# The opening of a hybrid encoder block on one core: a fixed order, block b11 of four token tiles first, two products of the second weight group brought forward, the normalised rows made twice instead of stored

## The chip, the core and the metric

The kernel runs on one core of one Trainium2 chip, in one launch. The metric is device time in microseconds; the median of three runs of the kernel before is 2131.55 us (2130.61 to 2132.82).

A core has TensorE (PE in the profile: matrix products and transposes, which accumulate into eight PSUM banks), VectorE (DVE), ScalarE (ACT) and GpSimd (POOL), each with its own instruction stream that is carried out in order, and DMA queues. In this kernel nearly all loads, and many stores, are issued by SyncE (SP), some by ACT.

## The reference, cut to what matters here

```python
h = layer_norm(x, ln_in_g, ln_in_b)          # x: 1024 tokens x 1024, fp32
proj = h @ w_in[l]                            # 1024 x (many column tiles of 128)
aq, ak, av, hq, hf_fwd, hf_bwd, hi, hg, ga, gh = jnp.split(proj, split_idx, axis=-1)
att = dilated_attention(aq, ak, av, slopes)
rec = hgrn2(hq, hf_fwd, hf_bwd, hi, hg, lower_bounds[:, l], hgrn_norm_g[l])
merged = sigmoid(ga) * (att @ w_att_up[l]) + sigmoid(gh) * (rec @ w_hgrn_up[l])
h = layer_norm(DEEPNORM_ALPHA * h + merged @ w_o[l], ln1_g[l], ln1_b[l])
gate, up = jnp.split(h @ w_ffn_in[l], 2, axis=-1)
h = layer_norm(DEEPNORM_ALPHA * h + (silu(gate) * up) @ w_ffn_out[l], ln2_g[l], ln2_b[l])
```

The change touches the first two lines, and the `DEEPNORM_ALPHA * h` of the first residual.

## The kernel before

**Phase 1** computes the transposed projection with a Winograd form of Strassen's product. The normalised and transposed x is a 2 x 2 matrix of blocks: b11 and b21 hold tokens 0 to 511 (token tiles 0 to 3), b12 and b22 hold tokens 512 to 1023 (tiles 4 to 7); b11 and b12 hold features 0 to 511, b21 and b22 the others. Four combinations are made: t1 = b12 - b11, t2 = b22 - t1, t3 = b22 - b12, t4 = b21 - b11 - t3 (which is b21 - t2). Each of the seven right-hand operands is kept as two fp32r tiles, a high part (a cast on ACT, L205) and a low part (a subtraction, L209, on DVE here). The weights of each *weight group* (four column tiles of 128, in two pairs g = 0 and 1) are loaded as blocks a11, a12, a21 and a22, and combined into s1 to s4.

**A product** is one of seven per pair and group, in the order a11·b11, a12·b21, s2·t2, s1·t1, s3·t3, s4·b22, a22·t4 (`ORDER` and `PRODUCTS`: 1, 2, 6, 5, 7, 3, 4), pair 0 and pair 1 of each in turn. It runs over four tiles of 128 features, and each takes three matmuls of 128 x 512 (`mm3`, L244 to L246): high by high, high by low, low by high. So a product is 12 matmuls.

**`stream` (L457)** is a generator that issues these products, one at each call. `block` loads a weight block on SP (L453) into a buffer of its own name and pair; there is one buffer for each, so a block of the next group is loaded once the last reader of the present one is done. `sums` makes s1 (L477, DVE), s3 (L478, POOL), s2 (L479, DVE) and s4 (L482, DVE) in place, five products ahead. `prep` splits a product's weights into high (ACT) and low (POOL) three products ahead. `keep` (L500) copies a partial sum out of PSUM on ACT, and the evacuations `plain`, `tanhs` and `silu2` (L390 to L420) add a kept sum to another one on DVE and store the outcome.

**`phase0` (L287)** prepares x, tile by tile: load (SP), statistics (L191 and L198 on DVE, epsilon L199 on DVE, power L200 on POOL), normalisation (L266 on DVE and L267 on ACT, the whole tile of 128 x 1024 at once), a store of the normalised rows `ah` through ACT's DMA queue (L317), then for each half of the features four transposes (L274, PE) into one PSUM bank, whose copies out (L282 on ACT, L284 on DVE) apply gain and offset. A tile of the first four fills its columns of b11 and of b21; a tile of the last four gives t1 and t2, and a loop at the end makes t3, b22 and t4 of those four tiles. `phase1` (L1088) lets it run for four tiles, then issues two products, then the rest of it; the products that follow come from the main loop of `phase1`, which mixes them with the attention and the recurrence (HGRN, L884 on).

**What sets the order.** Instructions are issued in the order in which the program issues them, but a list scheduler that simulates a timeline puts them into each engine's stream by priority and due time; `tc.high_priority(offset=evac_ahead)` raises evacuations and weight preparation.

**`residual` (L352)** runs much later, between two stretches of the last weight groups. For each token tile it loads the stored rows `ah` (L360, SP), scales them and adds the offset (L361 and L362, DVE), and stores the outcome (ACT's queue) for the first residual addition.

The lines of `residual`, `tanhs` and of the loop that calls `phase0` that the change and the steps touch:

```python
            nc.sync.dma_start(a, self.ah_d[tt])
            nc.vector.scalar_tensor_tensor(a, a, ALPHA, gb, op0=OP.mult, op1=OP.mult)
            nc.vector.scalar_tensor_tensor(a, bb, ALPHA, a, op0=OP.mult, op1=OP.add)
...
        work = self.stream(tiles)
            norm = self.phase0(p0)
            for _ in range(4):
                next(norm)
            for _ in range(2):
                next(work)
            for _ in norm:
                pass
```

Of the kernel before, what the change touches and what calls it, by code (L numbers as in the profile page):

```python
# [19 lines left out]
D = 1024  # L20
# [54 lines left out]
CST_PAD = 160  # L75
# [4 lines left out]
class Block:  # L80
    evac_ahead = 1000

    def __init__(self, ctx, tc, x, ln_in_g, ln_in_b, w_in, hgrn_lb, hgrn_norm_g, w_att_up, w_hgrn_up,
# [28 lines left out]
        self.ah_d = scratch("ah", 8)  # L112
# [25 lines left out]
    def consts(self):  # L138
# [20 lines left out]
        self.my = take(64).bitcast(I32)  # L159
        self.mhalf = cst.tile([128, 8], F32, name="mhalf")  # L160
        nc.vector.memset(self.mhalf, -0.5)

    def columns(self, pool):

        nc = self.nc
        rows = pool.tile([128, 128], F32, name="vrows")
        at, r = {}, 0
        for name, src, n in (("gin", self.ln["in"][0], 8), ("bin", self.ln["in"][1], 8), ("g1", self.ln["1"][0], 8),
                             ("b1", self.ln["1"][1], 8), ("lb", self.lbw, 32), ("ng", self.ng, 1)):
            nc.scalar.dma_start(rows[r:r + n, :], bass.AP(tensor=src.tensor, offset=src.offset, ap=[[128, n], [1, 128]]))  # L170
            at[name] = r
            r += n
        ps = self.ps_sd()
        nc.tensor.transpose(ps[:, :r], rows[:r, :], self.ident[:r, :r])
        a, b = self.cst.tile([128, 32], F32, name="vc"), self.cst1.tile([128, 33], F32, name="vc1")
        nc.vector.tensor_copy(a, ps[:, 0:32])
        nc.vector.tensor_copy(b, ps[:, 32:65])
        self.col = {n: a[:, at[n]:at[n] + 8] for n in ("gin", "bin", "g1", "b1")}
        self.lbraw, self.ngraw = b[:, 0:32], b[:, 32:33]

# [106 lines left out]
    def phase0(self, pool):  # L287


        nc, kept, rest = self.nc, [], []  # L290

        def hold(n):
            t = pool.tile([128, D], F32, name=n, tag="xt", bufs=7)
            return t, [t[:, HALF * i:HALF * (i + 1)].rearrange("p (k c) -> p k c", k=4) for i in range(2)]

        xs = []

        def load():
            tt = len(xs)
            if tt < 8:  # L300
                xs.append(hold("xt"))
                for h in range(2 if tt == 0 else 1):
                    s = slice(HALF * h, HALF * (h + 1)) if tt == 0 else slice(0, D)
                    nc.sync.dma_start(xs[tt][0][:, s], self.x[128 * tt:128 * (tt + 1), s])

        for tt in range(8):
            for _ in range(4 if tt == 0 else 1):
                load()
            xt, (t1, t2) = xs[tt]
            if tt == 0:  # L310
                self.columns(pool)
                gc, bc = self.col["gin"], self.col["bin"]
            if tt == 1:
                self.rest()
# [5 lines left out]
            def put(name, v, c=c):  # L320
                hi, lo = self.xb[name]
                self.split(hi[:, :, c], lo[:, :, c], v, eng_lo="dve")

            if tt < 4:
                v = [self.half3("v11"), self.half3("v21") if tt == 0 else
                     pool.tile([128, 4, 128], F32, name=f"v21{tt}")]
                kept.append(v)
                for q, n in enumerate(("b11", "b21")):
                    self.transposed(pool, xt, q, gc, bc, v[q], on_act=(1, 3, 4, 6))
                    put(n, v[q])  # L330
                yield
                continue
            b11, b21 = kept[tt - 4]
            _, (b12, b22) = hold("vt")
            self.transposed(pool, xt, 0, gc, bc, b12, on_act=(0, 1, 3))
            nc.vector.tensor_sub(t1, b12, b11)
            put("t1", t1)
            self.transposed(pool, xt, 1, gc, bc, b22, on_act=(4, 5, 7))
            nc.vector.tensor_sub(t2, b22, t1)
            put("t2", t2)  # L340
            rest.append((put, b12, b22, b21, b11))

        for put, b12, b22, b21, b11 in rest:
            nc.vector.tensor_sub(b12, b22, b12)
            put("t3", b12)
        for put, b12, b22, b21, b11 in rest:
            put("b22", b22)
        for put, t3, b22, b21, b11 in rest:
            nc.vector.tensor_sub(b21, b21, b11)
            nc.vector.tensor_sub(b21, b21, t3)  # L350
            put("t4", b21)

    def residual(self, pool, vecs):
# [95 lines left out]
    def block(self, n, g, name):  # L449

        t = self.blk.tile([128, 4, 128], F32, name=f"w{name}", tag=f"{name}{g}", bufs=1)
        c, r = self.cols[4 * n + 2 * g + int(name[1]) - 1], HALF * (int(name[2]) - 1)
        self.nc.sync.dma_start(t, self.w_in[r:r + HALF, c:c + 128].rearrange("(k p) c -> p k c", p=128))  # L453
        return t

    def stream(self, tiles):
# [3 lines left out]
        seq = [(n, g, p) for n in range(len(tiles) // 4) for p in self.ORDER for g in range(2)]  # L460
        after = {6: "a11", 7: "a21", 3: "a12", 4: "a22"}
        A = [{b: self.block(0, g, b) for b in ("a11", "a12", "a21", "a22")} for g in range(2)]
        state = [{}, {}]
        ready = {}

        def early(n):
            return tc.high_priority(offset=self.evac_ahead if n else 0)
# [27 lines left out]
        def bank(n, g, b):  # L495
            return self.ps_pj(2 * g + (n + b) % 2)
# [6 lines left out]
        for i in range(3):  # L503
            prep(i)
        for i, (n, g, p) in enumerate(seq):
            if i == 2:
                for j in range(4, 7):
                    sums(j)
                prep(4)
            if i >= 2:  # L510
                sums(i + 5)
            if i != 1:
                prep(i + 3)
            s = state[g]
            if p in (1, 2):
                s[p] = bank(n, g, p)
# [6 lines left out]
            pair = [f for _, f in tiles[4 * n + 2 * g:4 * n + 2 * g + 2]]  # L523
            with tc.high_priority(offset=self.evac_ahead):
                if p in (1, 6):
                    s["u"] = keep(ps, f"k1{g}")
                elif p == 5:
                    s["m5"] = keep(ps, f"k5{g}")
                elif p == 2:
                    pair[0](0, ps, s["u"])  # L530
                elif p == 7:
                    pair[1](1, ps, s["m5"])
                elif p == 3:
                    pair[0](1, ps, s["u"])
                else:
                    pair[1](0, ps, None)
# [551 lines left out]
    def phase1(self):  # L1088
# [12 lines left out]
        work = self.stream(tiles)  # L1101
        with self.pool("p0") as p0:
            norm = self.phase0(p0)
            for _ in range(4):
                next(norm)
# [620 lines left out]
```

## Time and profile before

| | |
|---|---|
| median of three runs | 2131.55 us |
| span of the profiled execution (no other time of it is recorded) | 2135.9 us |
| mean granted TensorE clock of that execution | 0.985 |
| TensorE busy in 84 to 200 us | 111.1 of 116 |
| TensorE busy in 200 to 1160 us | 929.2 of 960 |
| TensorE busy in 1160 to 1260 us, where the residual rows are made | 93.5 of 100 |
| TensorE busy from 1260 us on | 855.4 of 876 |

The span goes from the first to the last instruction of one profiled execution. It lies 4.3 us (0.2%) above the median of the runs, so numbers out of the trace are compared with numbers out of the trace, and differences are carried over to the median.

A row of the timeline gives the start in us, the duration in us, the engine, the line of the program, the operation, out<-in by the program's names, the tile's shape and type, and how many instructions the row holds; in brackets stands how long the engine was idle before, and which engine, tile and line released it. Matmuls overlap: a row's duration is that of its pipeline, and the distance between two starts is what one costs. Several instructions of one line in a row are put together (x8), and their duration then holds small gaps too. A row of the groups gives busy time and the mean in ns of one instruction, then the idle time ahead of such instructions and what ended most of it. A row of the windows gives the stretch, its length, then busy time and instruction count of PE, PE's weight loads, DVE, ACT and POOL, the granted clock, the share of the DMA engines' time and GB/s. Names in the trace are those of the buffers: `pj` and `sd` are PSUM banks, `wa` a weight block, `ws` a sum, `xt` and `vt` rows of x, `v` a transposed half tile, `evh` an evacuated half row.

### The profile page before, as it was taken

What the parts mean: (1) busy time and instruction counts of PE and PEld (TensorE: products, weight loads), DVE (VectorE), ACT (ScalarE), POOL (GpSimd) and SP (SyncE); (2) the same over time, 40 slices, a digit from 0 to 9 for tenths busy, and PEclk for the clock granted to TensorE, in tenths of its full rate; (3) what the DMA queues carried; (4) which work ended last, traced back from release to release, by engine and by line L of the source; (5) the groups of instructions that cost most, each with busy time, mean ns of one, the idle gap of its engine ahead of it and who ended that gap; (6) DMA issues with size and microseconds to landing.
All of it is one profiled execution on the core that took longest, in us unless ns stands there. A gap on an engine that the chain in (4) does not pass through costs nothing.

```text
span 2135.9 us, 30950 instructions
## 1 busy us (share of the span) xinstructions
PE 2032.5 (95%) x10941; PEld 1678.8 (79%) x10941; DVE 1386.7 (65%) x2228; ACT 918.9 (43%) x1864; POOL 1090.4 (51%) x882
## 2 busy tenths in 40 slices
PE   4799999999999999989999899999999999999998
PEld 3678787878878888868888688878788888888876
DVE  7666746776468754677536722336867677767777
ACT  6544445444554435443355332134433333334542
POOL 3465653565535764466644764353656666630012
PEclk9899999999999999999999999999999999999999
DMA  5343452434424453333433855244434334348433
GB/s 206 103 125 103 131 159 89 141 110 150 140 90 139 129 170 122 121 118 114 156 111 117 286 191 185 87 138 143 148 109 158 129 130 142 119 153 305 158 89 124
DMA packets 273885, 301.10 MB, mean 141 GB/s; under 512 B 14081, under 2 KB 205378, under 8 KB 273730
## 3 DMA queue, kind: packets, MB, share of 16 engines
q1 hardware_dynamic: 266272, 273.73, 39.9%
q10 hardware_dynamic: 7458, 25.40, 3.0%
q8 instruction: 86, 1.41, 0.3%
q14 instruction: 69, 0.57, 0.1%
HBM read 200.25 MB, written 98.83 MB: 140 GB/s over the span
## 4 chain that ended last, share of the span: by engine, by line
PE 62%; DVE 6%; issue 3%; DMA 3%; POOL 2%; ACT 1%; SPq 0%; ACTq 0%; DVEq 0%; POOLq 0%
PE pj L244 13%; PE pj L245 13%; PE pj L246 13%; PE sd L245 6%; PE sd L244 6%; PE sd L246 6%; POOL w_lo L209 1%; PE sd L1038 1%; PE sd L987 1%; DMA a<-ah 1%; DVE qd L956 1%; DVE qd L953 1%; POOL att_lo L209 0%; PE sd L643 0%; DVE hR L999 0%
## 5 line engine op out<-in xcount | busy, mean ns | idle before, releaser
L209 POOL TENSOR_TENSOR w_lo<-wa,w_hi 128x512 fp32r<-128x512 f32 x276 | 384.4, 1400 | 278.0 <-ACT w_hi L205 267.3
L205 ACT CAST w_hi<-wa 128x512 fp32r<-128x512 f32 x276 | 170.1, 618 | 231.1 <-PE pj L245 171.8
L209 POOL TENSOR_TENSOR w_lo<-wsum,w_hi 128x512 fp32r<-128x512 f32 x88 | 128.9, 1474 | 113.0 <-PE sd L246 60.7
L200 POOL TENSOR_TENSOR mv<-mv,mhalf 128x1 f32<-128x1 f32 x24 | 17.3, 723 | 228.9 <-DVE mv L199 225.7
L209 POOL TENSOR_TENSOR w_lo<-f_raw,w_hi 128x512 fp32r<-128x512 f32 x66 | 102.0, 1555 | 56.0 <-ACT w_hi L205 54.8
L244 PE MATMUL pj<-xt1hi,w_hi 128*128 128x512 f32 x260 | 105.0, 405 | 14.4 <-ACT xt1hi L205 6.9
L205 ACT CAST w_hi<-wsum 128x512 fp32r<-128x512 f32 x88 | 54.7, 621 | 124.6 <-PE sd L245 116.8
L245 PE MATMUL pj<-xt1lo,w_hi 128*128 128x512 f32 x260 | 103.5, 398 | 4.5 <-DVE xt1lo L209 4.5
L246 PE MATMUL pj<-xb22hi,w_lo 128*128 128x512 f32 x260 | 101.8, 391 | 1.6 <-POOL w_lo L209 1.6
L478 POOL TENSOR_TENSOR wa<-wa,wa 128x512 f32<-128x512 f32 x46 | 65.3, 1421 | 74.0 <-DVE ws L477 63.0
L246 PE MATMUL pj<-xt1hi,w_lo 128*128 128x512 f32 x260 | 102.9, 396 | 0.0
L244 PE MATMUL pj<-xb22hi,w_hi 128*128 128x512 f32 x260 | 102.5, 394 | 0.0
L245 PE MATMUL pj<-xb22lo,w_hi 128*128 128x512 f32 x260 | 101.8, 391 | 0.0
L209 POOL TENSOR_TENSOR w_lo<-ws,w_hi 128x512 fp32r<-128x512 f32 x46 | 67.3, 1467 | 64.2 <-ACT w_hi L205 63.9
L205 ACT CAST gwsum<-a_raw 128x512 fp32r<-128x512 f32 (+1 forms) x78 | 47.7, 616 | 100.9 <-PE pj L245 43.6
L500 ACT COPY wkeep<-pj 128x512 f32<-128x512 f32 x138 | 80.2, 581 | 11.4 <-DVE evh L392 5.9
L209 DVE TENSOR_TENSOR gwkeep<-a_raw,gwsum 128x512 fp32r<-128x512 f32 (+1 forms) x78 | 57.6, 739 | 41.1 <-ACT gwsum L205 38.2
L244 PE MATMUL pj<-xb11hi,w_hi 128*128 128x512 f32 x192 | 78.8, 412 | 4.9 <-DVE wkeep L417 3.4
L403 DVE TENSOR_TENSOR evh<-wkeep,pj 128x512 f32<-128x512 f32 x48 | 32.6, 680 | 76.4 <-PE pj L246 56.3
L244 PE MATMUL pj<-xt4hi,w_hi 128*128 128x512 f32 x192 | 77.1, 402 | 2.5 <-DVE evh L392 2.5
L246 PE MATMUL pj<-xt2hi,w_lo 128*128 128x512 f32 x192 | 75.7, 394 | 3.8 <-POOL w_lo L209 3.8
L990 ACT ACTIVATE hS<-hR,dec 128x128 f32<-128x128 f32 x112 | 44.5, 402 | 80.8 <-DVE hR L999 56.7
(406 smaller groups left out, 6608.3 us busy)
## 6 DMA issues: line engine op xcount, KB each, us to landing
wa<-in_w_in_dram SPq DMA_DIRECT2D x184, 256.0 KB, 3.1
f_raw<-in_w_ffn_in_dram SPq DMA_DIRECT2D x44, 512.0 KB, 4.2
a_raw<-gd SPq DMA_DIRECT2D x30, 512.0 KB, 3.8
gd<-fc SPq DMA_DIRECT2D x44, 256.0 KB, 2.0
gd<-fs SPq DMA_DIRECT2D x33, 256.0 KB, 2.1
tg<-evh SPq DMA_DIRECT2D x32, 256.0 KB, 2.9
tg<-tg SPq DMA_DIRECT2D x16, 512.0 KB, 3.8
y<-ahs SPq DMA_DIRECT2D x16, 512.0 KB, 5.3
```

What stands on the lines that cost most here:

```text
L205: nc.scalar.copy(hi, src)
L209: ins = e.tensor_sub(lo, src, hi.bitcast(F32))
L244: nc.tensor.matmul(ps, whi, xhi, start=first, stop=False, **kw)
L245: nc.tensor.matmul(ps, whi, xlo, start=False, stop=False, **kw)
L246: nc.tensor.matmul(ps, wlo, xhi, start=False, stop=last, **kw)
L403: nc.vector.tensor_add(t, add, ps)
L478: nc.gpsimd.tensor_sub(a["a21"], a["a11"], a["a21"])
L500: nc.scalar.copy(t, ps)
L953: nc.vector.reciprocal(qd[:, c, far], A[:, c])
L956: nc.vector.reciprocal(qd[:, c, near], R[:, c])
L987: nc.tensor.matmul(ps[:, jj, :], kT[b][:, c % 4, :], vT[:, c, :], start=True, stop=True)
L990: nc.scalar.activation(S[:, c, :], E, AF.Copy, scale=dec[:, 1, c:c + 1])
```

## The change

The opening gets an order written out by hand. `phase0` is no longer a generator: it is given the stream of products and issues, inside a region in which PE, DVE, ACT and POOL keep the program's order (`manual_schedule`), all preparation of x and the first 15 products. The order is: b11 of tiles 0 to 3; then b21 of tiles 0 to 3 with four products of b11 between them; then t1 and t2 of tiles 4 to 7 with the four products of b21; then the low and high parts of t1, t3, b22 and t4 with the products that follow. Evacuations of these products are collected in `held` and issued at chosen places (`done`).

In detail:

- A tile is normalised by halves of 512 columns. The statistics keep mean, 1/std and their product for each of the eight tiles in `mv0`; epsilon, power and the product are three small POOL operations (before: one on DVE, the power on POOL, one on DVE).
- t3 is subtracted on POOL, t4 is one subtraction from b21 (before two), tile 0's low part of b11 is made on POOL.
- The products go in the order (group 0, a11·b11), (group 1, a11·b11), (group 0, a12·b21), (group 1, a12·b21), the rest of group 0, the rest of group 1, and whole groups from the third on. For its first two products, group 1's a11 and a12 are loaded into `wfirst` tiles in the pool of the opening, three buffers for the four loads; for its sums they are loaded again into their usual buffers.
- Six buffers `xt` hold token tiles (before seven). The loads of x and of weight blocks are put in one fixed order on SP (`queued`).
- Some of the early products accumulate in `sd` banks instead of `pj` banks (`bank`).
- The loads of the vectors in `columns` come in two parts, the second one's transpose after the opening.
- The normalised rows are no longer stored. `residual` loads x again and normalises it once more with an ACT pass over 128 x 1024, from the kept `mv0`.

```diff
     def phase0(self, pool, work):
...
-            mv = self.stats(pool, xt, "0")
-            self.normalise(pool, xt, xt, mv)
-            nc.scalar.dma_start(self.ah_d[tt], xt)
...
+        def stats(tt):
+            st = self.tiny.tile([128, 2, 6], F32, name="bn0", tag="bnst", bufs=3)
+            for j in range(2):
+                nc.vector.bn_stats(st[:, j, :], xs[tt][0][:, HALF * j:HALF * (j + 1)])
+            mv = self.mv0[:, tt, :]
+            nc.vector.bn_aggr(mv[:, 0:2], st)
+            nc.gpsimd.tensor_scalar(mv[:, 2:3], mv[:, 1:2], LN_EPS, None, op0=OP.add)
+            nc.gpsimd.tensor_tensor(mv[:, 2:3], mv[:, 2:3], self.mhalf[:, 0:1], OP.pow)
+            nc.gpsimd.tensor_scalar(mv[:, 3:4], mv[:, 0:1], mv[:, 2:3], -1.0, op0=OP.mult, op1=OP.mult)
+
+        def norm(tt, q):
+            x, mv = xs[tt][0][:, HALF * q:HALF * (q + 1)], self.mv0[:, tt, :]
+            nc.scalar.activation(x, x, AF.Identity, bias=mv[:, 3:4], scale=mv[:, 2:3])
...
+        with self.tc.manual_schedule(engines={E.PE, E.DVE, E.Activation, E.Pool}):
...
+            norm(0, 0)
+            norm(0, 1)
+            turn(0, 0, v[0][0], (1, 3))
+            stats(1)
+            put(0, "b11", v[0][0], "pool")
+            norm(1, 0)
+            stats(2)
+            turn(1, 0, v[1][0], (1, 3))
+            norm(2, 0)
+            put(1, "b11", v[1][0])
+            stats(3)
+            turn(2, 0, v[2][0], (1, 3))
+            put(2, "b11", v[2][0])
+            norm(3, 0)
+            run()
+            turn(3, 0, v[3][0], (0, 1, 3))
+            put(3, "b11", v[3][0])
+            run()
+            for tt in range(4):
+                if tt < 3:
+                    norm(tt + 1, 1)
+                turn(tt, 1, v[tt][1], (1, 3))
+                put(tt, "b21", v[tt][1])
+                if tt:
+                    done()
+                if tt == 1:
+                    load(2)
+                if tt == 2:
+                    stats(4)
...
+                run()
+            for tt in range(4, 8):
+                b11, b21 = v[tt - 4]
+                norm(tt, 0)
+                norm(tt, 1)
+                t1, t2 = xs[tt][1]
+                _, (b12, b22) = hold("vt")
+                turn(tt, 0, b12, (0, 1, 3))
+                nc.vector.tensor_sub(t1, b12, b11)
+                if tt < 7:
+                    stats(tt + 1)
+                turn(tt, 1, b22, (0, 1, 3))
+                nc.vector.tensor_sub(t2, b22, t1)
+                put(tt, "t2", t2)
+                nc.gpsimd.tensor_sub(b12, b22, b12)
+                nc.vector.tensor_sub(b21, b21, t2)
+                v[tt] = t1, b12, b22, b21
+                done()
+                if tt > 4:
+                    late(tt - 1, 0)
+                run()
...
-            nc.sync.dma_start(a, self.ah_d[tt])
+            nc.sync.dma_start(a, self.x[128 * tt:128 * (tt + 1), :])
+            mv = self.mv0[:, tt, :]
+            nc.scalar.activation(a, a, AF.Identity, bias=mv[:, 3:4], scale=mv[:, 2:3])
...
-        seq = [(n, g, p) for n in range(len(tiles) // 4) for p in self.ORDER for g in range(2)]
+        O = self.ORDER
+        order = [(n, (p,)) for p in O[:2] for n in (0, 1)]
+        order += [(n, O[2:] if n < 2 else O) for n in range(len(tiles) // 4)]
+        seq = [(n, g, p) for n, part in order for p in part for g in range(2)]
...
+            if n == 1 and p == 2:
+                first[g, 2] = self.block(1, g, "a12", pool)
...
-                self.split(*ready[i], A[g][self.PRODUCTS[p][0]])
+                self.split(*ready[i], first[g, p] if n == 1 and p < 3 else A[g][self.PRODUCTS[p][0]])
```

In this diff `turn` transposes a half tile and copies it out (its last argument names the four copies that ACT makes), `put` splits a half tile into high and low, `late` splits t1, t3, b22 or t4 of a tile, `run` issues the next step of the stream (from the fourth call on, a product), and `done` the next held evacuation.

More of the change, by code (lines that the diff above doesn't have):

```diff
@@ L1 @@
 import math
+from functools import partial
 from contextlib import ExitStack
@@ L343, in phase0 @@
[L343 to L351, printed above, removed]
+                    self.queued(xs[tt][0][:, s], self.x[128 * tt:128 * (tt + 1), s])
+        def stats(tt):
[7 more added lines that the diff above has]
+            nc.gpsimd.tensor_scalar(mv[:, 3:4], mv[:, 0:1], mv[:, 2:3], -1.0, op0=OP.mult, op1=OP.mult)
@@ L353, in residual @@
+        held, self.held = self.held, None
+        for f in held:
+            f()
+        for _ in cols:
+            pass
     def residual(self, pool, vecs):
@@ L522, in stream @@
                          skip_group_check=True)
[L523 to L536, printed above, removed]
+            done = partial(self.leave, tiles[4 * n + 2 * g:4 * n + 2 * g + 2], p, ps, s, keep,
+                           f"k{5 if (n, p) == (1, 1) else 1}{g}", f"k5{g}")
+            if self.held is None:
+                done()
+            else:
+                self.held.append(done)
             yield 4 * n + 2 * g + 2 if p == 4 else 0
@@ L1100, in phase1 @@
         self.cst1 = side.enter_context(self.pool("cst1"))
[L1101 removed]
         with self.pool("p0") as p0:
[L1103 to L1109 removed]
+            work = self.stream(tiles, p0)
+            self.phase0(p0, work)
         self.hgrn_setup()
```

192 lines of the change are left out of this document (116 added, 76 removed).

## The prediction

> **What bounds the kernel now.** I read the busy times first, then the opening in a table of two windows.
>
> ```profile
> span 2135.9 us, 30950 instructions
> ...
> PE 2032.5 (95%) x10941; PEld 1678.8 (79%) x10941; DVE 1386.7 (65%) x2228; ACT 918.9 (43%) x1864; POOL 1090.4 (51%) x882
> ```
>
> ```profile
> 0.00:42.00 42.00, 13.27 (x47) 8.68 (x47) 30.21 (x80) 23.45 (x42) 14.50 (x26) 1.00 0.69 243
> 42.00:84.00 42.00, 30.16 (x118) 24.00 (x119) 32.87 (x55) 27.85 (x57) 15.79 (x13) 0.84 0.15 51
> ```
>
> TensorE is busy for 95% of the span, and the edited stage holds a large part of what is missing: 43.4 of the first 84 us. Whatever lets matmuls run earlier there moves the end one for one, as long as nothing starves later. Next, TensorE's timeline of the opening.
>
> ```profile
> 42.46 0.79 PE L245 MATMUL pj<-xb11lo,w_hi 128*128 128x512 f32 x1 [1.00 <-DVE xb11lo L209]
> 43.05 0.63 PE L246 MATMUL pj<-xb11hi,w_lo 128*128 128x512 f32 x1
> 43.48 0.63 PE L244 MATMUL pj<-xb11hi,w_hi 128*128 128x512 f32 x1
> ...
> 57.36 0.60 PE L274 MATMUL sd<-tabs_sb,xt 128*128 128x128 f32 x4
> 64.87 1.22 PE L244 MATMUL pj<-xt1hi,w_hi 128*128 128x512 f32 x2 [6.92 <-ACT xt1hi L205]
> 70.56 0.79 PE L245 MATMUL pj<-xt1lo,w_hi 128*128 128x512 f32 x1 [4.47 <-DVE xt1lo L209]
> ...
> 83.28 0.39 PE L244 MATMUL pj<-xb22hi,w_hi 128*128 128x512 f32 x1
> 83.50 0.39 PE L245 MATMUL pj<-xb22lo,w_hi 128*128 128x512 f32 x1
> ```
>
> A product is 12 matmuls. They start 0.43 us apart after idleness (43.05, 43.48) and 0.227 apart when warm (83.28, 83.50): 5.1 or 2.7 us. Products start at 42.5, wait 6.9 and 4.5 us for t1, and at 83.28 eight are done. **83.28 is my yardstick**: the changed kernel also has eight products (b11 and b21 of two weight groups) before the first product of t2.
>
> **The change, step by step.** In the built order all four engines now stand in program order in the opening, so the time is a chain of hand-offs. Prices:
>
> ```profile
> 4.07 1.41 DVE L191 BATCH_NORM_STATS2 bn<-xt 128x6 f32<-128x512 f32 x2 [3.20 <-DMA xt<-in_x_dram]
> 5.51 0.21 DVE L198 BATCH_NORM_AGGREGATE mv<-bn 128x2 f32<-128x12 f32 x1
> ...
> 5.99 0.55 POOL L200 TENSOR_TENSOR mv<-mv,mhalf 128x1 f32<-128x1 f32 x1 [3.13 <-DVE mv L199]
> ...
> 34.62 1.11 PE L274 MATMUL sd<-tabs_sb,xt 128*128 128x128 f32 x4 [4.31 <-ACT v L282]
> ...
> 35.34 0.40 DVE L284 TENSOR_SCALAR v<-sd,vc 128x128 f32<-128x128 f32 x1
> ...
> 35.77 0.46 ACT L282 ACTIVATE v<-sd,vc 128x128 f32<-128x128 f32 x1 [1.21 <-DVE v L284]
> ```
>
> ```profile
> L191 DVE BATCH_NORM_STATS2 bn<-xt 128x6 f32<-128x512 f32 x16 | 10.3, 675 | 5.8 <-DMA xt<-in_x_dram 5.8
> ...
> L336 DVE TENSOR_TENSOR xt<-vt,v 128x512 f32<-128x512 f32 x4 | 2.7, 678 | 0.0
> ```
>
> ```profile
> L267 ACT ACTIVATE xt<-xt,mv 128x1024 f32<-128x1024 f32 x8 | 9.9, 1241 | 6.9 <-DVE mv L266 6.9
> L282 ACT ACTIVATE vt<-sd,vc 128x128 f32<-128x128 f32 x24 | 9.7, 459 | 1.5 <-PE sd L274 0.9 <-DVE vt L284 0.6
> ...
> L500 ACT COPY wkeep<-pj 128x512 f32<-128x512 f32 x6 | 3.5, 578 | 0.0
> ...
> L205 ACT CAST xt2hi<-xt 128x512 fp32r<-128x512 f32 x4 | 2.5, 622 | 2.9 <-DVE xt L339 2.9
> ...
> L404 ACT ACTIVATE evh<-evh 128x512 f32<-128x512 f32 x1 | 0.6, 643 | 0.0
> ```
>
> ```profile
> L1043 POOL TENSOR_SCALAR hss<-hss 128x4 f32<-128x4 f32 x16 | 3.7, 231 | 16.6 <-DVE hss L1042 16.2
> ```
>
> A consumer starts 0.03 us after its producer's row ends (35.34 + 0.40, then 35.77). The four copies of a half tile out of PSUM alternate DVE, ACT, DVE, ACT: 0.43 + 0.49 + 0.43 + 0.46 = 1.8. Statistics of a tile are 1.3; the small POOL chain now holds three operations (0.23 + 0.55 + 0.23, the two outer ones by L1043): 1.1. A half normalise, which the trace of before does not show, lies between the 0.46 copy of 128 columns and the whole normalise of 1024 (1.24, L267); I take 0.64, an ACT pass over 512 columns (L404). Back to back on one engine, instructions overlap by 0.08 to 0.1, so a subtraction costs 0.6 there and a cast 0.53.
>
> *b11 of four tiles.* Statistics end at 5.72, POOL 6.8, normalise 7.45, transposes 8.6, copies 10.4. Tile 1: its statistics stand behind those copies on DVE (11.2), then 1.1 + 0.64 + 1.11 + 1.8: 15.9. Tile 2 is normalised by 16.5, but DVE first makes tile 1's low part (17.9) and tile 3's statistics (19.2), so its copies end at 21.0. Tile 3: cast 21.6, normalise 22.3, transposes 23.4, three weight casts on ACT to 24, copies 25.8, cast and low part 27. First product: 26, against 42.5. This part does what the change says. On SP, tiles 6 and 7 and the last two wfirst loads wait for the transposes of tiles 0 and 1 to free their buffers (32 and 35); with 3.7 us from load to use (row at 92.19, below) for the last of them they are there by 40 and wanted after 46: nothing.
>
> *b21.* One product at 5.1 and three at 2.7 with transposes between them (0.6 each): to 41.7. Tile 3's b21 copies could follow, but DVE has tile 2's low part (to 41.4), tile 4's statistics (1.3), a weight sum (0.7), a wait for POOL's three small operations and a subtraction (1.1 + 1.3) and a second weight sum (0.7) ahead of them: 46.5. Copies, cast: 49; product five (cold again) to 54, tile 4's transposes (in order behind it) to 55.
>
> *t2 of four tiles.* From the end of a tile's transposes: copies ACT, ACT, DVE, ACT 1.75; DVE t1 0.6, next statistics 1.3, copy 0.43; ACT copy 0.49; DVE t2 0.7: the ACT cast starts at 5.3. For tiles 5 and 6 there follow DVE low part, t4 subtraction and evacuation (0.6 + 0.6 + 0.7), and on ACT tanh, t1 cast, weight cast (0.53 apart), and only then the next normalise (0.64) and transposes (1.11): 11.3 a tile. Tile 4 has no evacuation: 8.7. Tile 7 needs no statistics: 4.7 to its cast. POOL's t3 subtraction is freed together with t2:
>
> ```profile
> 27.82 2.50 POOL L209 TENSOR_TENSOR w_lo<-wa,w_hi 128x512 fp32r<-128x512 f32 x2 [2.18 <-ACT w_hi L205]
> 29.30 1.57 DVE L209 TENSOR_TENSOR xb21lo<-v,xb21hi 128x512 fp32r<-128x512 f32 x1
> ```
>
> The DVE subtraction took 1.57 instead of 0.68 and ended 0.55 us after POOL's at 30.32: they took turns. I add 0.6 to tiles 5 and 6 (0 if they never meet, 1.3 if POOL goes first). The Trainium skill's GPSIMD Engine Reference (1. Specifications) speaks against the four subtractions given to POOL: POOL shares its SBUF interfaces with DVE instructions of two SBUF inputs. The rows agree; by the rule each of the four could hold back a DVE step, 5 us in all.
>
> Eighth product behind us, t2 ready: 55 + 8.7 + 2 x 11.9 + 4.7 = 92, against 83.28: **+8.7** (bounds: warm transposes at 0.60 and no collisions +4; POOL always first +11). TensorE has idled, so the restart is cold:
>
> ```profile
> 117.67 0.47 PE L244 MATMUL pj<-xt1hi,w_hi 128*128 128x512 f32 x1 [1.60 <-DVE wkeep L417]
> ...
> 125.72 0.47 PE L244 MATMUL pj<-xt1hi,w_hi 128*128 128x512 f32 x1 [3.31 <-DVE evh L403]
> ...
> 126.57 0.63 PE L244 MATMUL pj<-xt1hi,w_hi 128*128 128x512 f32 x1
> ...
> 129.89 0.39 PE L246 MATMUL pj<-xt1hi,w_lo 128*128 128x512 f32 x1
> ```
>
> From 126.57 to 129.89 eight matmuls ran 0.2 slower each: **+1.6**.
>
> *Group 1 brought forward.* Its first two products use extra loads (wfirst, 4 x 256 KB, landed early), but its next one (s2) needs a22, whose buffer group 0 gives back only at its last products. Before, six products of slack lay between; now four fewer, and the built order even puts group 1's product ahead of group 0's last. Before, that refill ran so:
>
> ```profile
> 86.48 0.62 ACT L205 CAST w_hi<-wa 128x512 fp32r<-128x512 f32 x1 [2.12 <-PE pj L245]
> ```
>
> ```profile
> 88.53 2.58 SPq L453 DMA_DIRECT2D wa<-in_w_in_dram  x2
> ```
>
> ```profile
> 92.19 0.69 DVE L477 TENSOR_TENSOR ws<-wa,wa 128x512 f32<-128x512 f32 x1 [4.78 <-DMA wa<-in_w_in_dram]
> ```
>
> ```profile
> 92.96 1.30 POOL L478 TENSOR_TENSOR wa<-wa,wa 128x512 f32<-128x512 f32 x1 [2.24 <-DVE ws L477]
> ```
>
> From the cast to the sum 5.7 us, of which load to sum 3.7. On DVE the evacuation of the first t3 product now stands behind that sum: cast to sum 5.7, POOL's subtraction 2.1, second sum and evacuation 1.4, tanh 0.65, two casts of t4 1.1, low part 0.7: 11.7 after the t3 product, while TensorE has three products (8.2): idle 3.5. The second a22 follows: load to sum 3.7, 2.1, 1.4 behind the low weights (1.3), against 5.4 of products: idle 2.9. With about 1.5 cold restarts, 2.4: **+9** (0 if group 1's loads come from elsewhere in time, 11).
>
> *Recurrence behind it.* The 1.60 and 3.31 waits at 117 and 125, with their cold restart (6.5 in all), are evacuations queued behind the recurrence on DVE. Since TensorE is now held earlier, my layout has those scans done before the evacuations are due: **-6.5** (bound 0).
>
> *Not stored, made twice.* Eight stores leave ACT's queue, hidden now. In the residual stage each row gets one more ACT pass (1.24 by L267's size), before DVE:
>
> ```profile
> 1196.23 3.05 DVE L361 SCALAR_TENSOR_TENSOR a<-a,ginb 128x1024 f32<-128x1024 f32 x1 [5.70 <-DMA a<-ah]
> ```
>
> ```profile
> PE pj L246 <- POOL w_lo L209: 4.8, 4, 1.7
> PE pj L244 <- DVE evh L403: 1.5, 1, 1.5
> ```
>
> Here DVE waits on the load, evacuations and weight casts stand behind, and TensorE already loses 6.3 us. One pass is on the chain at 1196, the others wait among idle ACT time: **+1.5** (0 to 5; without that cover 8 x 1.24).
>
> Everything else stands in the old order. Sum: 8.7 + 1.6 + 9 - 6.5 + 1.5 = **+14.3**. The profiled execution went from 2135.9 to 2150.2 so; its span is 4.3 over the runs' median of 2131.55, to which I add the same: **2146**.
>
> **Rivals.** *A, the busiest engine sets the pace.* If neighbouring tiles overlap in spite of the order, ACT decides: up to the last t2 cast 16 half normalises x 0.64 + 41 copies x 0.46 + 26 casts x 0.62 + 4 keeps x 0.58 + 2 tanh x 0.65 = 49, and with a table load and a tenth of waiting t2 is ready at 61. Then 61 - 83.3 + 1.6 + 9 - 6.5 + 1.5 = -17.7: 2114. For it: before, DVE was busy for 33 and ACT for 28 of the second 42 us, so such work can be packed. Against it: on ACT one tile's t2 cast, tanh and t1 cast stand ahead of the next tile's normalise. It decides from 6 us a tile instead of 11 (14.3 us less over three tiles). *B, the refill is in time*: without the 9 us 2137. *C, no recovery*: the recurrence stalls as before, POOL always wins, 14.3 + 6.5 + 2.5 = +23: 2155.
>
> **How the numbers follow.** Forecast (2141 to 2151) 0.43, A (2105 to 2126) 0.17, B (2133 to 2141) 0.18, C (2151 to 2162) 0.20; the rest 0.02. The range 2127 to 2160 leaves out A and the edge of C. Of 2131.55, 0.2% is 4.3 us, what a measurement of this kernel can tell from no change: below 2127.3 A and its neighbours, 0.18; within, the lower part of B, 0.10; slower 0.72.
>
> **What would show it.** First product near 26; the first matmul of t2 near 92 (below 78 my hand-offs are wrong and A holds); transposes of tiles 5, 6 and 7 some 9 to 12 apart; two gaps of about 3 us ahead of the t4 products, released by the evacuation of a t3 product and by the one behind the next sum; no waits of the kind at 117 and 125; one or two us more idle TensorE between 1180 and 1240. Wrong it would be if DVE or ACT showed no idle time between tiles 5 and 7.

## The result, and the profile after

The changed kernel takes 2159.02 us (median, 2156.0 to 2162.14), the kernel before 2132.19 us beside it: ratio 1.0121, 95% interval 1.0106 to 1.0136, or 26 us (23 to 29) slower. The profiled execution went from a span of 2135.9 to 2156.6.

The head of the page after:

```profile
span 2156.6 us, 30934 instructions
...
PE 2040.9 (95%) x10942; PEld 1681.1 (78%) x10942; DVE 1379.8 (64%) x2203; ACT 931.9 (43%) x1881; POOL 1095.3 (51%) x903
```

The windows of the opening after (columns as in the prediction):

```profile
0.00:42.00 42.00, 19.02 (x72) 14.35 (x73) 14.35 (x31) 20.30 (x36) 15.30 (x32) 1.00 0.57 177
42.00:84.00 42.00, 22.62 (x76) 16.92 (x75) 24.19 (x38) 19.72 (x40) 14.48 (x19) 0.69 0.03 10
84.00:100.00 16.00, 7.20 (x22) 5.06 (x21) 9.19 (x15) 8.06 (x16) 5.71 (x6) 0.61 0.04 16
```

TensorE starts earlier, as intended: 19.0 us busy of the first 42, against 13.3. In the next 42 it drops from 30.2 to 22.6, and between 84 and 100, where before it had no gap, it is idle for more than half. In the second stretch no other engine is busy for more than 24 of 42 us, while DVE had 33 before: the opening has become a chain in which the engines wait for each other.

TensorE's timeline after, the rows behind its waits:

```profile
27.38 0.79 PE L253 MATMUL pj<-xb11hi,w_hi 128*128 128x512 f32 x1 [2.72 <-ACT xb11hi L214]
...
52.89 0.80 PE L253 MATMUL sd<-xb21hi,w_hi 128*128 128x512 f32 x1 [9.04 <-ACT xb21hi L214]
...
58.23 1.03 PE L283 MATMUL sd<-tabs_sb,xt 128*128 128x128 f32 x8
...
66.69 1.97 PE L283 MATMUL sd<-tabs_sb,xt 128*128 128x128 f32 x8 [4.67 <-ACT xt L327]
...
78.83 1.97 PE L283 MATMUL sd<-tabs_sb,xt 128*128 128x128 f32 x8 [3.71 <-ACT xt L327]
...
90.99 1.97 PE L283 MATMUL sd<-tabs_sb,xt 128*128 128x128 f32 x8 [4.59 <-ACT xt L327]
...
96.94 0.80 PE L253 MATMUL pj<-xt2hi,w_hi 128*128 128x512 f32 x1 [3.99 <-ACT xt2hi L214]
...
125.23 0.49 PE L253 MATMUL pj<-xt4hi,w_hi 128*128 128x512 f32 x1 [2.99 <-ACT xt4hi L214]
...
133.47 0.50 PE L253 MATMUL pj<-xt4hi,w_hi 128*128 128x512 f32 x1 [0.31 <-DVE evh L468]
...
159.60 0.47 PE L253 MATMUL pj<-xt4hi,w_hi 128*128 128x512 f32 x1 [0.85 <-DVE wkeep L493]
...
167.79 0.76 PE L253 MATMUL pj<-xb11hi,w_hi 128*128 128x512 f32 x1 [3.57 <-DVE wkeep L493]
```

(L283 are the transposes, L327 the half normalises, L253 to L255 the three matmuls.) The rows tell the story: the first product at 27.4; 9 us of waiting for the last part of b21; then the transposes of tiles 4 to 7 at 58.2, 66.7, 78.8 and 91.0; the first product of t2 at 96.9, where the ninth product before was at 83.28: 13.7 us late. Behind it TensorE waits again at 125, 160 and 168.

To see what is lost when this is over, a landmark that every version has: the two copies of the recurrence's second head out of PSUM, in ACT's timeline before and after.

```profile
224.47 1.07 ACT L577 COPY hv<-sd 128x512 f32<-128x512 f32 x2
```

```profile
249.35 1.08 ACT L686 COPY hv<-sd 128x512 f32<-128x512 f32 x2
```

So 24.9 us are lost by then, of 26.8 between the two medians. (The two spans differ by 20.7: that of the kernel before lies 4.3 above its median, that of the changed kernel 2.4 below its own.) To within some us the cause lies in the opening, and in what it does to the 150 us that follow.

### The profile page after: what moved, and what is told of

Same layout as the page of the kernel before. It is cut to its first block, busy times and chain, and to the rows that moved or that the text cites. A ratio compares the mean times of both kernels' runs of the same rounds, so it can differ in the third digit from the quotient of the medians.

```text
span 2156.6 us, 30934 instructions
## 1 busy us (share of the span) xinstructions
PE 2040.9 (95%) x10942; PEld 1681.1 (78%) x10942; DVE 1379.8 (64%) x2203; ACT 931.9 (43%) x1881; POOL 1095.3 (51%) x903
## 5 line engine op out<-in xcount | busy, mean ns | idle before, releaser
L218 POOL TENSOR_TENSOR w_lo<-wa,w_hi 128x512 fp32r<-128x512 f32 x272 | 377.4, 1394 | 284.0 <-ACT w_hi L214 273.1
L209 POOL TENSOR_TENSOR mv<-mv,mhalf 128x1 f32<-128x1 f32 x16 | 10.8, 678 | 207.0 <-DVE mv L208 206.9
L253 PE MATMUL pj<-xt1hi,w_hi 128*128 128x512 f32 x252 | 99.8, 396 | 3.2 <-DVE evh L468 2.7
L253 PE MATMUL pj<-xb22hi,w_hi 128*128 128x512 f32 x252 | 99.3, 394 | 0.0
L255 PE MATMUL pj<-xb22hi,w_lo 128*128 128x512 f32 x252 | 98.6, 391 | 0.0
L254 PE MATMUL pj<-xt1lo,w_hi 128*128 128x512 f32 x252 | 98.6, 391 | 0.0
L255 PE MATMUL pj<-xt1hi,w_lo 128*128 128x512 f32 x252 | 98.4, 391 | 0.0
L253 PE MATMUL pj<-xb11hi,w_hi 128*128 128x512 f32 x192 | 80.7, 420 | 9.9 <-DVE wkeep L493 5.8
L253 PE MATMUL pj<-xt2hi,w_hi 128*128 128x512 f32 x192 | 78.3, 408 | 8.6 <-ACT wkeep L618 4.6
L253 PE MATMUL pj<-xt4hi,w_hi 128*128 128x512 f32 x192 | 78.7, 410 | 7.7 <-DVE evh L468 3.8
L254 PE MATMUL pj<-xb11lo,w_hi 128*128 128x512 f32 x192 | 78.6, 409 | 0.3 <-DVE xb11lo L218 0.3
```

Of the source, the lines that this page charges most:

```text
L209: nc.gpsimd.tensor_tensor(mv[:, 2:3], mv[:, 2:3], self.mhalf[:, 0:1], OP.pow)
L218: ins = e.tensor_sub(lo, src, hi.bitcast(F32))
L253: nc.tensor.matmul(ps, whi, xhi, start=first, stop=False, **kw)
L254: nc.tensor.matmul(ps, whi, xlo, start=False, stop=False, **kw)
L255: nc.tensor.matmul(ps, wlo, xhi, start=False, stop=last, **kw)
```

## The experiments

Of the changed kernel, unless said otherwise. "Delay" is the landmark of the run's trace less 224.47 (two traces of programs that are alike up to there differ by 0.4, the changed kernel and e4, and by 1.0, the kernel before and e9); "time" is what the ratio to the kernel before, taken beside it, makes of 2133 us.

| | delay at the landmark | time against before, us (95%) |
|---|---|---|
| the changed kernel | +24.9 | +26 (23 to 29) |
| e1, sums later | +18.3 | +22 (18 to 25) |
| e2, normalise earlier | +17.8 | +18 (15 to 22) |
| e3, evacuation before sums | +17.0 | +23 (19 to 27) |
| e4, no second pass | +25.3 | +25 (22 to 28) |
| e7, e1 to e3 together | +14.5 | +18 (15 to 21) |
| e5, not brought forward | +20.5 | +26 (23 to 29) |
| e6, order lifted | -7.0 | -4.3 (-6.2 to -2.1) |
| e13, order lifted, not brought forward | -7.9 | -4.3 (-6.2 to -2.3) |
| e10, order on TensorE alone | +1.4 | +5.3 (3.0 to 7.7) |
| e12, order on ACT alone | +4.8 | +6.6 (3.8 to 9.2) |
| e11, order on DVE alone | +17.9 | +23 (19 to 26) |

**e1: the wait of 9 us.** DVE's timeline after shows what stood ahead of the copies that TensorE waited for:

```profile
43.66 0.69 DVE L218 TENSOR_TENSOR xb21lo<-v,xb21hi 128x512 fp32r<-128x512 f32 x1 [1.18 <-ACT xb21hi L214]
44.27 1.28 DVE L318 BATCH_NORM_STATS2 bn<-xt 128x6 f32<-128x512 f32 x2
...
45.70 0.64 DVE L591 TENSOR_TENSOR ws<-wa,wa 128x512 f32<-128x512 f32 x1
48.70 1.73 DVE L593 TENSOR_TENSOR wa<-ws,wa 128x512 f32<-128x512 f32 x1 [2.35 <-POOL wa L592]
50.36 0.40 DVE L293 TENSOR_SCALAR v<-sd,vc 128x128 f32<-128x128 f32 x1
```

The transposes of tile 3 had ended at 43.9. Their first copy starts at 50.36, behind tile 4's statistics and two weight sums, with 2.35 us in which DVE stands still for POOL. The edit moves both behind tile 3:

```diff
-                if tt == 2:
-                    stats(4)
                 if tt == 3:
+                    stats(4)
...
+            if i in (4, 5):
+                sums(i + 4)
-            if not late:
+            if not late and i not in (3, 4):
                 sums(i + 5)
```

> The weight sums of group 0 and the statistics of tile 4 now stand behind tile 3's part of b21 on DVE. Theory (the order of hand-offs holds TensorE): the 9.0 us wait ahead of the first product of b21 (43.9 to 52.9) shrinks to about 2.5 (four copies 1.8, a cast 0.6), the first product of t2 starts near 90.5 in place of 96.9, and the time falls by 5 to 6.5 us. Rival (the work is only moved: DVE or ACT sets the pace): the sums then delay tile 4, t2 starts no earlier than 95, and the time falls by less than 2.

The first product of b21 starts at 46.50, after a wait of 2.98; that of t2 at 92.18, 4.8 earlier:

```profile
46.50 0.80 PE L253 MATMUL sd<-xb21hi,w_hi 128*128 128x512 f32 x1 [2.98 <-ACT xb21hi L214]
...
92.18 0.80 PE L253 MATMUL pj<-xt2hi,w_hi 128*128 128x512 f32 x1 [3.99 <-ACT xt2hi L214]
```

The mechanism is as the theory had it, and the delay falls by 6.6 us at the landmark. The median falls by only 2 (2157.05), less than forecast, and the intervals of the two kernels overlap. The executions of one kernel scatter by 3 to 11 us, so the landmark is the better yardstick for what an edit of this size does up to there. That its gain reaches the end is not shown: e1, e3, e5 and e11 are 4.4 to 7.9 us ahead of the changed kernel at the landmark and 2 us ahead or less in time (see the last section).

**e2: from tile to tile.** ACT's timeline after between tiles 5 and 6:

```profile
76.41 0.63 ACT L480 ACTIVATE evh<-evh 128x512 f32<-128x512 f32 x1 [2.50 <-DVE evh L479]
76.94 0.60 ACT L214 CAST xt1hi<-xt 128x512 fp32r<-128x512 f32 x1
...
77.97 1.52 ACT L327 ACTIVATE xt<-xt,mv 128x512 f32<-128x512 f32 x2
```

From 73.9 on ACT has nothing to do that its order allows, and the normalise of tile 6, whose statistics were long there, waits for a tanh whose operand DVE has not yet made. The edit:

```diff
-                norm(tt, 0)
-                norm(tt, 1)
+                if tt == 4:
+                    norm(4, 0)
+                    norm(4, 1)
...
                 put(tt, "t2", t2)
+                if tt < 7:
+                    norm(tt + 1, 0)
+                    norm(tt + 1, 1)
```

> On ACT the two half normalises of tiles 5, 6 and 7 stand ahead of the evacuation's tanh, the t1 cast and the weight cast of the tile before. Theory: the distance between the transposes of tiles 4 to 7 (8.5, 12.1, 12.2) falls to 8 to 9 each, t2 starts near 89, and the time falls by 6 to 8 us. Rival (DVE's own work of a tile sets the distance): it stays above 11, and the time falls by less than 2.

```profile
65.20 1.97 PE L283 MATMUL sd<-tabs_sb,xt 128*128 128x128 f32 x8 [3.70 <-ACT xt L327]
...
73.82 0.79 PE L283 MATMUL sd<-tabs_sb,xt 128*128 128x128 f32 x4
75.42 0.63 PE L283 MATMUL sd<-tabs_sb,xt 128*128 128x128 f32 x4 [0.81 <-DVE evh L483]
...
79.06 0.79 PE L253 MATMUL sd<-xb21hi,w_hi 128*128 128x512 f32 x1 [3.02 <-ACT vt L291]
...
84.35 0.65 PE L283 MATMUL sd<-tabs_sb,xt 128*128 128x128 f32 x4
85.94 0.63 PE L283 MATMUL sd<-tabs_sb,xt 128*128 128x128 f32 x4 [0.94 <-DVE wkeep L497]
...
92.69 0.79 PE L253 MATMUL pj<-xt2hi,w_hi 128*128 128x512 f32 x1 [6.12 <-ACT xt2hi L214]
```

Part of what the theory said: the first transposes of tiles 5, 6 and 7 start at 65.20, 73.82 and 84.35, so the distances fall to 8.6 and 10.5, the second one not to 8 or 9; t2 starts 4.3 earlier, the time falls by 5.6 us. New waits have taken the place of the old one. The second half of a tile's transposes now waits for an evacuation on DVE (0.81, 0.94), and the product that follows for copies on ACT (3.02): the products of b21 accumulate in the `sd` banks, and the transposes need such banks too.

**e3: the refill.**

```diff
-                    if tt % 2:
+                    if tt % 2 and i < 3:
                         run()
                         done()
+            for _ in range(2):
+                done()
+                run()
```

> The evacuation of the first t3 product and the low parts of t4 stand ahead of group 1's weight sums on DVE. Theory (group 1's refill of a22 costs through that order): TensorE's waits of 2.99 and 0.31 us at 125 are gone, with the cold matmuls behind them: 4 to 5 us less at the first t4 product, and 3 to 5 less in all. Rival (given back at the waits behind the recurrence at 160 and 168): the wait at 125 goes but the time falls by less than 1.

The wait ahead of the first t4 product is gone, but 3.08 us come back one product later, behind a weight cast:

```profile
125.48 0.47 PE L253 MATMUL pj<-xt4hi,w_hi 128*128 128x512 f32 x1 [3.08 <-ACT w_hi L214]
```

The waits behind the recurrence shrink but are not gone: 0.19, 1.89 and 0.65 us at 151, 159 and 166, 2.7 in place of 4.4 (DVE's first scan starts at 135.5 in place of 144.3). The delay is 7.9 less at the landmark, 2.3 of it from t2, which started at 94.61 in this execution. The median is that of the changed kernel (2158.63). Which theory the run speaks for is not clear: the trace is with the first, the time with the second.

**e7: the three together.**

> The three moves that were tried one by one (weight sums later, normalises earlier, evacuation before group 1's sums) together. Theory: they lie at three places of one chain and add up: t2 starts at 84 to 88, the delay against the kernel before falls from 24 us at 200 us to 4 to 8 there, and the time is 2139 to 2147. Rival (gains of the opening are given back behind 200 us): the delay at 200 us falls as much, but the time stays above 2150.

```profile
88.84 0.79 PE L253 MATMUL pj<-xt2hi,w_hi 128*128 128x512 f32 x1 [6.12 <-ACT xt2hi L214]
...
119.86 0.47 PE L253 MATMUL pj<-xt4hi,w_hi 128*128 128x512 f32 x1 [2.98 <-ACT w_hi L214]
...
157.51 0.77 PE L253 MATMUL pj<-xb11hi,w_hi 128*128 128x512 f32 x1 [4.23 <-DVE wkeep L499]
```

They don't add up. t2 comes 8.1 earlier (4.8 and 4.3 would be 9.1), but the recurrence's wait is longer again (4.23), and the delay is 14.5 where the theory had 4 to 8; the time is 2153.11. The theory falls; of the rival, the time came true and the delay did not. There are not three faults in an otherwise good order: where a gap is closed, the next one shows.

**e6: the order lifted.** The same instructions (each engine has as many as in the changed kernel), with one line changed:

```diff
-        with self.tc.manual_schedule(engines={E.PE, E.DVE, E.Activation, E.Pool}):
+        with ExitStack():
```

> The fixed order is lifted: the same instructions, but the list scheduler orders the four engines in the opening. Theory (the hand-offs of the fixed order hold TensorE): t2 starts before 90 in place of 96.9, and the time falls by 6 us or more. Rival (the data's own dependencies and the work of DVE and ACT set it): t2 starts within 3 us of 96.9 or later, the time falls by less than 2.

2129.88 us: 29 less than the changed kernel, and faster than the kernel before (ratio 0.998, interval 0.9971 to 0.999). TensorE's last transposes here and what follows, and the stretch that holds those of tiles 4 to 7, here and in the changed kernel:

```profile
64.99 1.11 PE L283 MATMUL sd<-tabs_sb,xt 128*128 128x128 f32 x4 [4.21 <-DVE evh L479]
73.33 1.22 PE L253 MATMUL sd<-xt1hi,w_hi 128*128 128x512 f32 x2 [7.22 <-ACT xt1hi L214]
...
78.59 1.22 PE L253 MATMUL pj<-xt2hi,w_hi 128*128 128x512 f32 x2 [3.76 <-ACT xt2hi L214]
```

```profile
46.00:76.00 30.00, 15.03 (x75) 11.50 (x74) 27.59 (x42) 22.69 (x49) 13.29 (x8) 0.78 0.16 53
```

```profile
58.00:97.00 39.00, 20.09 (x71) 15.02 (x69) 22.50 (x37) 20.73 (x42) 13.13 (x16) 0.67 0.04 14
```

The last transposes are done at 66, not at 93. DVE is busy for 27.6 of 30 us, where it had 22.5 of 39: the work of neighbouring tiles overlaps, and I read this as a busy engine that sets the pace instead of a chain of hand-offs. The waits at 125, 160 and 168 are gone as well; between 100 and 200 us TensorE waits 1.2 us for POOL and 0.9 for DVE.

**e10, e11, e12: which engine's order.** The fixed order kept on one engine, the three others left to the scheduler: `engines={E.PE}`, `{E.DVE}`, `{E.Activation}`.

> The fixed order holds on TensorE alone; the scheduler orders DVE, ACT and POOL. Between the changed kernel (2159) and the one with the order lifted (2130) lie 29 us. Theory (the order of ACT and DVE makes the chain from tile to tile): TensorE's order alone costs less than 6 us of them, time 2127 to 2136. Rival (transposes that stand behind products on TensorE make it): 15 or more, 2145 to 2159.

> The fixed order holds on DVE alone. Theory: it costs 8 to 18 us of the 29, since sums, statistics and evacuations stand ahead of copies that are ready (tile 3's b21 copies again start some 5 us late or more): 2138 to 2148. Rivals: under 4 (ACT's order is all), 2126 to 2134; or 25 and more (DVE's order is all), 2155 to 2160.

> The fixed order holds on ACT alone. Theory: it costs 12 to 25 us of the 29, since each tile's normalise stands behind the tanh and the t1 cast of the tile before, which wait for DVE: tiles 5 to 7 follow each other in 9 to 12 us, 2142 to 2155. Rivals: under 4 (DVE's order is all), 2126 to 2134; or all of it, 2155 to 2160.

2139.6, 2157.31 and 2140.92. DVE's order alone costs 27 of the 29 us, more than my theory gave it: the rival (DVE's order is all) was right. ACT's costs 11 and TensorE's 10, the first a little under and the second above what was expected. They don't add (48 for 29), as if each held the same chain. POOL's order alone was not tried, nor the order lifted on DVE alone. With DVE's order alone TensorE shows the old pattern:

```profile
54.45 0.80 PE L253 MATMUL sd<-xb21hi,w_hi 128*128 128x512 f32 x1 [9.26 <-ACT xb21hi L214]
...
76.86 0.63 PE L283 MATMUL sd<-tabs_sb,xt 128*128 128x128 f32 x4 [1.81 <-ACT xt4hi L214]
...
87.67 0.63 PE L283 MATMUL sd<-tabs_sb,xt 128*128 128x128 f32 x4 [2.08 <-ACT xt4hi L214]
92.89 1.22 PE L253 MATMUL sd<-xt1hi,w_hi 128*128 128x512 f32 x2 [4.59 <-ACT xt1hi L214]
```

The 9 us ahead of b21 are back, tiles 6 and 7 are 10.8 apart although ACT may normalise whenever it likes, and t1 starts at 92.9.

**e5 and e13: without the products brought forward,** under the fixed order and with it lifted.

```diff
-        order = [(n, (p,)) for p in O[:2] for n in (0, 1)]
-        order += [(n, O[2:] if n < 2 else O) for n in range(len(tiles) // 4)]
-        seq = [(n, g, p) for n, part in order for p in part for g in range(2)]
+        seq = [(n, g, p) for n in range(len(tiles) // 4) for p in self.ORDER for g in range(2)]
```

(The steps of the stream, the held evacuations, the weight sums and the loads of tiles 6 and 7 are called at other places, to fit.)

> Nothing of the second weight group is brought forward: the products go group by group as before the change, the rest of the fixed opening stays. Theory (the four extra products fill TensorE, but their evacuations, tanh passes and sd banks stand in the very hand-offs that set the pace): the transposes of tiles 4 to 7 follow each other in 8 to 10 us in place of 12, t2 starts at 82 to 88 in place of 96.9, four products (10.9 us) come later, the waits at 125 are gone, and the time stays within 4 us of the changed kernel's. Rival 1 (the products brought forward are a free filling): t2 starts as late as before, and the time rises by 8 to 11. Rival 2 (bringing forward is what made it slow): the time falls by 10 or more.

> The fixed order is lifted, and nothing of the second weight group is brought forward. Theory (with the order lifted, TensorE has idle time ahead of t2 that the four products fill): t2 or t1 starts no more than 4 us earlier, four products (10.9 us) come later, and the time is 5 to 11 us above that with the products brought forward: 2135 to 2141. Rival (bringing forward gives nothing, as it gave nothing under the fixed order): within 3, 2127 to 2133.

2159.7 and 2130.06: the same as with them, 2159.02 and 2129.88. Under the fixed order the time is as the theory had it, and the waits at 125 are gone. The rest is not: the tiles follow each other in 11.1, 11.6 and 8.5 us and not in 8 to 10, and t2 starts at 92.99, 4 us earlier, and not at 82 to 88. With the order lifted my theory is wrong: t1 starts 6.8 earlier (66.54), and bringing forward gives nothing. So four products that fill a gap in one place are paid for in another; that they are paid with their evacuations, tanh passes and banks is likely, and not shown.

**e4 and e9: the residual stage.** In e4 the line of the second pass in `residual` is left out:

```diff
-            nc.scalar.activation(a, a, AF.Identity, bias=mv[:, 3:4], scale=mv[:, 2:3])
```

> The second normalisation in the residual stage is left out (its rows are those of x itself, so the first residual gets raw x). Theory (the pass stands on the chain of that stage): the 4.6 us wait of TensorE behind ACT near 1246 is gone, and the time falls by 2 to 4 us. Rival (ACT has idle time there, the pass is hidden): less than 1.

2161.04 us, no gain: the rival was right. TensorE's waits in that stage, of the changed kernel and of e4:

```profile
PE pj L253 <- ACT wkeep L618: 4.6, 1, 4.6
PE pj L255 <- POOL w_lo L218: 1.3, 2, 0.9
PE pj L253 <- DVE evh L479: 1.3, 2, 1.0
```

```profile
PE pj L255 <- POOL w_lo L218: 5.7, 5, 1.7
PE pj L253 <- DVE evh L478: 1.6, 1, 1.6
```

7.2 and 7.3 us: without the pass TensorE waits as long, for another engine. e9 is the kernel before with the residual rows' stores (ACT's queue) issued by SP.

> The kernel before, with the stores of the residual rows issued by SP and no longer by ACT (where each stands in ACT's order until DVE has made its row: 8.2 us at 1217 to 1226). Theory (the 6.3 us that TensorE waits in this stage come from that order): the time falls by 2 to 5 us against the kernel before. Rival (SP's loads then stand behind the stores): no gain, or up to 3 us slower.

2136.78 us, ratio 1.0019 (1.0009 to 1.0029): a little slower. TensorE waits 6.8 us in the stage, before 6.3. Taking the stores out of ACT's order brings nothing; the theory falls.

## Why the prediction was right, point by point

The direction and the cause were right: hand-offs in a fixed order, t2 late. The size was not: +14 us were forecast and +27 measured. 2159 lies inside the range (2127 to 2160) by 1 us, and in the band that the prediction gave to rival C (2151 to 2162), not in that of the forecast itself (2141 to 2151). By its steps, with the sum at the landmark:

- **b11 and b21.** First product forecast at 26, measured 27.4 (the second matmul waits to 28.5). The products of b11 that run between b21's tiles end 1.5 us later than forecast (43.2). Tile 3's b21 was mis-sized: 49 against 52.9. Of these 3.9, 2.9 are there when tile 2's low part ends on DVE (44.3 against 41.4). For the rest the step saw the right instructions in front of it (statistics, two sums, POOL); it gave the second sum 0.7 where it took 1.73, and POOL's four operations 2.4 where they took 2.8 (45.88 to 48.67 in POOL's timeline).
- **The tiles' distance.** Forecast 8.7, 11.9, 11.9; measured 8.5, 12.1, 12.2. These are the starts. So t2 is 13.7 late and not 8.7, and 4.3 of that 5 was there when tile 4's transposes ended (59.3 against 55).
- **The cold restart.** 1.6 forecast. The first product of t2 took 5.65 us (96.94 to 102.59) and not 2.7: 2.9, of which 0.2 is a wait.
- **The refill.** The first gap is there, 2.99 and 0.31 against 3.5, released by the t4 cast as worked out. The second, forecast at 2.9 (its terms give 3.1), is 0.31; why it is so short was not looked into. With cold matmuls about 5 in place of 9.
- **The recurrence: the step that failed.** "My layout has those scans done before the evacuations are due", -6.5. It was worth nothing: the scans were put off more than TensorE was. DVE's first one starts at 144.3 where it started at 101.7, 42.6 us later, while t2 is 13.7 late, and the same queueing came back at 160 and 168 (0.85 and 3.57).
- **The residual stage.** +1.5 forecast; e4 shows nothing that can be measured, the lower bound.

The first scan, in the kernel before and in the changed one:

```profile
101.69 1.21 DVE L942 TENSOR_TENSOR_SCAN fa<-fa,d 128x512 f32<-128x512 f32 x1
```

```profile
144.32 1.22 DVE L1051 TENSOR_TENSOR_SCAN fa<-fa,d 128x512 f32<-128x512 f32 x1 [7.17 <-ACT fa L1039]
```

Two things put it off, the order and the products brought forward: it starts at 109.0 without the order (e6), at 125.1 without the products (e5) and at 97.6 without both (e13). And taking away DVE's order or the products is enough to end nearly all of the queueing. TensorE's longest wait for DVE between 100 and 200 us is 0.94 in e6 and 0.29 in e10 and e12, where DVE's order is lifted, and 0.34 in e5, where it is fixed and nothing is brought forward (2.4 in e11, which has both):

```profile
166.87 0.47 PE L253 MATMUL pj<-xb11hi,w_hi 128*128 128x512 f32 x1 [0.34 <-DVE evh L481]
```

From the ninth product (83.28 before, 96.94 after) to the landmark both traces hold 710 matmuls, before and after:

```profile
83.28:224.47 141.19, 135.56 (x710) 112.92 (x709) 96.11 (x107) 60.44 (x112) 89.94 (x77) 0.99 0.40 127
```

```profile
96.94:249.35 152.41, 142.75 (x710) 116.57 (x711) 109.61 (x137) 67.59 (x128) 89.03 (x82) 0.95 0.39 125
```

So the 24.9 us are 13.7 of a later start, 4.0 more of waits (9.7 against 5.6) and 7.2 that the same number of matmuls took longer, at a granted clock of 0.95 against 0.99. The terms above place 13.7 + 2.9 + 5 + 0 = 21.6 of them; the other 3 are not put down to single waits. That the time came out inside the range is in part luck: two errors of opposite sign (5 too little in the opening, 4 too much in the refill) nearly cancelled, and the recovery that did not come (6.5) is half of the 13 us by which the forecast was short.

Of the rivals, C ("no recovery", 2155) is the nearest, in time and in its main part, the recurrence that stalls as before. A is what the same instructions do once the order is lifted, as its condition said (neighbouring tiles overlap): t2 starts at 78.6, and not at its 61, and the time is 2130, not 2114 (its terms add up to -16.7 and not -17.7, so 2115). What makes e6 4 us faster than the kernel before was not taken apart; it isn't the bringing forward.

## What to carry to other kernels

An order written out by hand is a promise on every engine at once: each instruction that waits holds all that stand behind it, however ready. When no engine is busy for more than some 60% of a stretch and TensorE still waits (as here from 42 to 84 us), look for what stands ahead of the ready work in the engine that hands over most (here DVE), and try the order lifted before shaping its parts. Here lifting it on all four engines was worth 29 us, DVE's order alone cost 27, and three careful repairs inside the order brought 6; that lifting DVE's alone would do was not tried. Work that is brought forward to fill a gap brings its evacuations and buffers with it; price these where they land.

## What the runs showed of the hardware

The granted clock goes to one half in whole steps of 3.4 us after a wait, and the number of steps differs: behind the wait of 0.85 us at 160 none, behind that of 2.99 at 125 one, behind that of 3.57 at 168 two. The last two in windows of the changed kernel:

```profile
126.20:129.60 3.40, 3.40 (x9) 2.64 (x10) 0.00 (x0) 0.65 (x2) 2.33 (x6) 0.50 0.27 79
167.10:173.90 6.80, 6.11 (x17) 4.98 (x17) 6.80 (x9) 3.07 (x6) 3.89 (x3) 0.50 0.21 77
```

The Trainium skill's TensorE: Matmul & The Clock Gate (Part 1: The HAM clock gate) says that the gate works in free-running windows of about 3.4 us that do not begin with the kernel; the lengths here agree.

The same wait is not always followed by as many steps. Up to 1160 us the kernel before and e9 run the same lines: a wait of 1.87 us at 679 was followed by one step in the one trace and by none in the other, and a wait of 4.0 us at 954 by two and by one. Added up over each trace's clock records from 200 us on (without the last, which runs past the end), where the programs differ little, the half clock held for 31 to 44 us, and it costs up to half its length (matmuls of a product start 0.43 us apart in place of 0.227), so some 6 us between the traces. The eleven times of e6 go with the clock: 2131.72 to 2135.35 us at a mean of 0.984, 2128.47 to 2129.91 at 0.985 and 0.986, 2126.05 at 0.987. With this scatter a gain of 5 us in the opening can be seen at a landmark of the trace and hardly in four times.

Not all of the gap between landmark and time need be scatter. In e3's trace the half clock held for 10 us less than in the changed kernel's before 200 us, and for 10 us more behind it; and the mean clock of its four runs, 0.977 to 0.979, is no higher than the changed kernel's (0.977 to 0.980). Whether an edit in the opening also moves waits behind the landmark into more half-clock steps was not looked into.
